# Two heads on the two halves of the array: float32 attention products reordered beside long split products

## The chip, the core and the metric

The kernel runs as one program on one core of a Trainium2 chip. TensorE multiplies (in the trace PE, with its weight loads as PEld), VectorE (DVE) and ScalarE (ACT) do the elementwise work, GpSimd (POOL) and SyncE (SP, which issues DMAs) help. The metric is the device time of one execution in microseconds: the median of three timed runs. A second, separate execution was profiled; all rows below come from that one.

## The reference, cut to what matters

Two transformer blocks with 256 tokens and a model width of 2048. The first block (run for two layers) mixes a state-space scan with an attention of eight heads, whose queries and keys have a part of 128 and a rotary part of 64; the scores are the sum of both parts:

```
q = jnp.concatenate([q[..., :MLA_NOPE], apply_rope(q[..., MLA_NOPE:], cos, sin)], axis=-1)   # 128 + 64
s = jnp.einsum('bqhd,bkhd->bhqk', q[:, q0:kend], k[:, :kend]) * scale     # causal, blocks of 128 queries
outs.append(jnp.einsum('bhqk,bkhd->bqhd', p, v[:, :kend]))
```

The second block has a branch with 16 query heads of width 64 in four key groups. Its output is a gated sum of three attentions:

```
o_cmp = jnp.einsum('bsgrc,bcgd->bsgrd', p_cmp, vc)         # over 15 block summaries per group
o = g[..., 0:1] * o_cmp + g[..., 1:2] * o_sel + g[..., 2:3] * o_win
```

With 256 tokens the selected blocks and the window each cover every causal key, so `o_sel` and `o_win` are plain causal attentions over two sets of keys and values. A second branch of that block, with heads of width 128, is not touched.

## The kernel before, in words

**Long products.** Nearly all work is products of the 256 tokens with weights of width 2048 and more. Weights and activations are split into a high and a low part; `block` (L423 to L425) issues three products of 128x512 for every slice of 128 rows, `block_fm` (L461 to L463) three of 128x256. A weight tile arrives by DMA (`raw`), ACT makes its high part `wh` (L411), DVE its low part `wl` (L412). There are five `raw` buffers and four of `wh` and of `wl`; these steps are put far ahead of the others by priority.

**Tasks.** The rest is written as generators that the long products advance: `tick` is called every six products of `block`, and each task then issues its next step and says how many ticks it wants to wait (`yield n`). PE's order is exactly the order in which the program is written out this way; DVE, ACT and POOL are ordered by a scheduler with priorities.

**Attention of a head.** `scores` (L665) writes the scores of the two query tiles into one PSUM bank `[128, 384]`: 256 keys for the second tile, 128 for the first. `soft` (L627 to L633) makes the exponentials from it: DVE writes `z`, ACT the exponential `e`, and `scaled` (L647) applies 1/sum and the gate. `probs_t` (L653 to L655, copied by ACT at L657) transposes `e`. Then the values' products. `z`, `e` and the transposed probabilities are tiles of a ring of nine buffers, `t2`; the PSUM banks `mb` are a ring of four.

**The two users that change.** `mla_heads` (first block, four pairs of heads in each of two layers) issues the scores of head 0 in one tick and those of head 1 in the next; per query tile a product over 128 rows (`qn`, `kk`) and one over 64 rows (`rp`, rows 0 to 63 for head 0, 64 to 127 for head 1). `branch_a_heads` (second block, eight chunks of two heads, a new chunk every seven ticks) issues four scores over 64 rows in four ticks: head 0 with both key sets, then head 1. For each head then follow two transposes, two ticks later four products of 64 columns of values (L1493, L1494), and one product of 15 rows, the block summaries (L1496).

**How the trace names it.** A float32 product of the program appears as two passes, each with its own weight load: L665 with `kt,qt` is issued 64 times and has 128 records. A form such as `64*128 64x256` reads: weights of 64 rows by 128 columns, a moving operand of 64 rows by 256 columns.

Of the kernel before, what the change touches and what calls it, by code (L numbers as in the profile page):

```python
# [15 lines left out]
OP = mybir.AluOpType  # L16
# [3 lines left out]
P = 128  # L20
# [14 lines left out]
# ---------------------------------------------------------------- host layout  # L35
# [6 lines left out]
def _tile_a(w, width=512):  # L42
    """[L, K, N] -> [L, N/width, K/512, 2, 128, 2, width]; one [128, 2, width] block per transfer."""
    L, K, N = w.shape
    w = w.reshape(L, K // 512, 2, 2, P, N // width, width)
    return np.ascontiguousarray(w.transpose(0, 5, 1, 2, 4, 3, 6))


def _tile_b(w):
    """[L, 2048, N] -> [L, N/128, 2, 128, 8, 128]."""  # L50
    L, K, N = w.shape
    w = w.reshape(L, 2, 8, P, N // P, P)
    return np.ascontiguousarray(w.transpose(0, 4, 1, 3, 2, 5))


def _cols(v):
    """[n*128] -> [128, n]"""
    return v.reshape(-1, P).T


def _rows(v):
    """[n] -> [128, n], the same row on every partition"""
    return np.broadcast_to(v.reshape(1, -1), (P, v.size))


def _feature_major(x):
    """[256, 2048] -> [128, 16, 256]"""
    return np.ascontiguousarray(x.T.reshape(16, P, S).transpose(1, 0, 2))


def _token_major(x):
    """[256, n] -> [128, 2, n]"""
    return np.ascontiguousarray(x.reshape(2, P, -1).transpose(1, 0, 2))
# [19 lines left out]
def _head_order_a():  # L93
    """Position p of a query head of branch a: pairs (g, g + 1) of key groups with one r."""
    return [(2 * (c // 4) + i) * 4 + c % 4 for c in range(8) for i in range(2)]
# [64 lines left out]
def _layout(a):  # L160
    """Every array that goes to the chip, in the order and the shape it is read."""
    o = {}
# [11 lines left out]
    L = DEPTH  # L174
# [48 lines left out]
# ---------------------------------------------------------------- the program  # L223


class _Task:
    """Work beside the long products, cut into steps; a step yields the number of ticks to wait."""
# [5 lines left out]
class _Net:  # L233
# [29 lines left out]
    # -- tasks  # L263
# [17 lines left out]
    def get(self, t):  # L281
        """the result of a task, a list of them, or the value itself"""
        if isinstance(t, _Task):
            while not t.done:
                self.tick()
            return t.result
        return t
# [6 lines left out]
    # -- small things  # L294
# [30 lines left out]
    def rsqrt(self, out, ss, width):  # L325
        """out = (ss / width + eps) ** -0.5"""
# [9 lines left out]
    def squares(self, src, acc):  # L336
        """acc = sum of src ** 2 along the free axis"""
        self.nc.scalar.activation(self.junk[:, :src.shape[1]], src, AF.Square, accum_out=acc)

    def head_squares(self, src, acc, heads):  # L340
        """acc [128, heads] = sum of squares of every head's columns of src [128, 512]"""
# [4 lines left out]
    # -- operands of the long products  # L346
# [6 lines left out]
    def hi_lo(self, pair, c, n, src, gain=None, imm=None):  # L353
        """chunks c .. c+n of a pair from src [128, n, 256], times a gain by partition"""
# [17 lines left out]
    def two_transposed(self, srcs):  # L372
        """srcs: two functions of the token tile giving [128 tokens, 128]; a bank [128, 2, 256]"""
# [9 lines left out]
    def transposed(self, src, gain=None, imm=None):  # L383
        """src(m) -> [128 tokens, 512]; a task for its four chunks, feature-major, as a pair"""
# [8 lines left out]
    def weights(self, src, n, w):  # L393
        """one block [128, n, w] from DRAM, split into high and low parts"""
# [19 lines left out]
    def block(self, pairs, srcs, w=512, hold=HOLD):  # L414
        """token-major products: two banks [128 tokens, w]; the last weights serve one bank, then the other"""
# [35 lines left out]
    def block_fm(self, pairs, src):  # L451
        """feature-major products for 128 columns: one bank [128 features, 256 tokens]"""
# [15 lines left out]
    # -- the residual stream  # L468
# [24 lines left out]
    # -- start  # L493

    def start(self):
        """the first operands, in the order they are needed"""
# [44 lines left out]
    def angles(self):  # L541
        """cosines and sines of every rotary embedding"""
# [45 lines left out]
    def rope_gains(self, l, which):  # L588
        """rotary tables with the gain of the rotated part folded in"""
# [12 lines left out]
    def rotate(self, out, x, ct, st):  # L602
        """out, x [128, ..., 2 * half] (up to three free axes), tables broadcast to the same shape"""
# [12 lines left out]
    # -- attention of one head  # L616

    def soft(self, s, mask, scale_of, spans):
        """spans [(lo, hi)] by query tile over the columns of a bank; returns exp and 1/sum"""
# [29 lines left out]
    def probs_t(self, e):  # L649
        """probabilities [128, 384] transposed: keys by [tile 0: all tokens | tile 1: second half]"""  # L650
# [9 lines left out]
    def scores(self, s, parts):  # L660
        """s [128, 384]; parts [(qT [k, 256], kT [k, 256])] sum over the contraction"""
        nc = self.nc
        for m, (a, b) in reversed(list(enumerate(self.CAUSAL))):
            for i, (q, k) in enumerate(parts):
                nc.tensor.matmul(s[:, a:b], lhsT=q[:, m * P:(m + 1) * P], rhs=k[:, 0:b - a],  # L665
                                 start=(i == 0), stop=(i == len(parts) - 1))

    # ------------------------------------------------------------ block 1
# [72 lines left out]
    def rms_bank(self, r):  # L741
        """a column by token tile, as rows on every partition"""
# [13 lines left out]
    def ssd_steps(self, l, krd):  # L756
        """softplus of the step sizes, and the decays by step"""
# [48 lines left out]
    def ssd_scan(self, l, cb, dt, a):  # L806
# [24 lines left out]
        # masked c . b, state positions on the partitions  # L831
# [9 lines left out]
        # state after the first chunk  # L841
# [19 lines left out]
        def decays(m, g):  # L861
            """rows of summed decays for 8 heads"""
# [84 lines left out]
    def mla_queries(self, l, qa_t, rqa):  # L947
        """[nope heads 0-3, nope heads 4-7, rope of all heads] before the norm; -scale/rms by (tile, head)"""
# [68 lines left out]
    def mla_heads(self, l, hp, q, nsc, kn, kr, v):  # L1017
        """two heads: chunks of the pair that four heads share"""
# [12 lines left out]
        es = []  # L1031
        for j in range(2):
            h = hp * 2 + j
            s = self.bank([P, 384])
            b = slice(j * 64, j * 64 + 64)
            self.scores(s, [(qn[:, j], kk[:, j]), (rp[b, 0], rp[b, 1])])
            e, rc = self.soft(s, self.causal, lambda m: nsc[:, m, h:h + 1], self.CAUSAL)
            self.scaled(e, rc)
            es.append(e)
            yield 1  # L1040
        yield 3
# [15 lines left out]
    # -- attention to the memory  # L1057
# [34 lines left out]
    def head_rms(self, t, name):  # L1092
        """t [128, 2, 512]: 1/rms by (tile, head of 128)"""
# [84 lines left out]
    # -- feed forward  # L1178
# [45 lines left out]
    # ------------------------------------------------------------ block 2  # L1224
# [29 lines left out]
    def x_fm(self, nb):  # L1254
        """512 features of x times their gain, feature-major"""
# [9 lines left out]
    def h2_pair(self, nb, xt, rb):  # L1265
        """512 features of rms(x) * g_pre * (1 + scale) + shift"""
# [19 lines left out]
    def rope_part(self, t, c0, heads, dh, rot, tabs):  # L1286
        """rotate the first rot of every head's dh columns of t[:, :, c0:...] in place"""
# [3 lines left out]
    def gate_fm(self, pairs, src):  # L1291
        """twice silu of 4 feature-major chunks"""
# [10 lines left out]
    def plain_t(self, src, out):  # L1303
        """out [128, 4, 256] = four chunks of src(m), feature-major"""
# [5 lines left out]
    def summaries(self, t, c0, which, vc):  # L1310
        """block summaries of the columns c0.. (4 groups of 64) of t: [128 (group, 32), 64]"""
# [70 lines left out]
    def branch_a_inputs(self, pairs):  # L1382
# [11 lines left out]
        # a quarter of 1 + tanh: the gate, halved against the doubled silu  # L1394
# [7 lines left out]
    def branch_a_cmp(self, tasks, qt, ga, kcr):  # L1402
        """probabilities over the block summaries, gated: [128 (group, 32), r, tokens]"""
        nc = self.nc
        for t in tasks:
            yield from self.after(t)
        x = kcr[:, 0:16].unsqueeze(1)
# [50 lines left out]
    def branch_a_heads(self, c, kts, qt, ks, kt, ga, cmp, vcr, zf):  # L1458
        """the two query heads of chunk c"""
# [9 lines left out]
        for i in range(2):  # L1469
            g = 2 * gp + i  # L1470
            b = slice(i * 64, i * 64 + 64)
            for br in range(2):
                s = self.bank([P, 384])
                self.scores(s, [(qt[gp][b, r], kt[b, 2 * br + gp])])
                e, rc = self.soft(s, self.causal, lambda m: -0.125, self.CAUSAL)
                f = self.small([P, 2], name="fa")
                nc.vector.tensor_tensor(f, rc, ga[:, :, (br + 1) * 16 + r * 4 + g], op=OP.mult)
                self.scaled(e, f)
                es[i, br] = e
                yield 1  # L1480
        yield 1
        o = self.bank([P, S])
        for i in range(2):
            g = 2 * gp + i
            b = slice(i * 64, i * 64 + 64)
            vs = slice(256 + g * 64, 256 + (g + 1) * 64)
            pts = []
            for br in range(2):
                pts.append(self.probs_t(es[i, br]))
                yield 1  # L1490
            yield 1
            for br, t in enumerate(ks):
                nc.tensor.matmul(o[b], lhsT=t[:, 0, vs], rhs=pts[br][:, 0:256], start=(br == 0), stop=False)  # L1493
                nc.tensor.matmul(o[b, P:], lhsT=t[:, 1, vs], rhs=pts[br][:, 256:384], start=False, stop=False)  # L1494
            cs = slice(g * 32, g * 32 + 15)
            nc.tensor.matmul(o[b], lhsT=vcr[cs], rhs=pct[cs, r], start=False, stop=True)  # L1496
# [6 lines left out]
    def branch_b(self, pairs, nb):  # L1503
        """inputs of 4 heads"""
# [8 lines left out]
    def branch_b_heads(self, h, q, k, v, zf):  # L1513
# [9 lines left out]
        self.scores(s, [(qk[:, 0], qk[:, 1])])  # L1523
# [16 lines left out]
    def gate_rows(self):  # L1540
        """gate * g_post along the free axis"""
# [13 lines left out]
    def hybrid(self, xt, r):  # L1555
# [7 lines left out]
        vcr = self.small([P, 64], name="vcr", bufs=1)  # L1563
        qt, qts = [], []
# [9 lines left out]
        cmp = self.spawn(self.branch_a_cmp(qts + [cmp], qt, ga, kcr), 1)  # L1574
        za = [self.gate_fm(pairs, I["w2_za"][0, c:c + 4]) for c in (0, 4)]
        oa = [self.spawn(self.branch_a_heads(c, kts, qt, ks, kt, ga, cmp, vcr, za), 1 + A_LAG * c) for c in range(8)]
# [101 lines left out]
```

## Time and profile before

| what | value |
|---|---|
| median of three timed runs | 3197.31 us (3196.97 to 3197.81) |
| profiled execution, first to last instruction (its span) | 3196.7 us; the page gives no other time for it |
| PE busy | 3175.3 us, 99% of the span, 15705 matmul records |
| PE weight loads busy | 2656.9 us |
| DVE, ACT, POOL busy | 2034.1, 1553.8, 53.4 us |
| mean granted clock | 0.998 of 2.4 GHz |

A PE that is busy all the time is not a PE at its peak: a matmul's recorded time includes the part in which the next one already streams. What a product costs in a row of products is the distance from its start to the next start, and the rows below are read that way.

### The profile page before, as it was taken

What the parts mean: (1) busy time and instruction counts of PE and PEld (TensorE: products, weight loads), DVE (VectorE), ACT (ScalarE), POOL (GpSimd) and SP (SyncE); (2) the same over time, 40 slices, a digit from 0 to 9 for tenths busy, and PEclk for the clock granted to TensorE, in tenths of its full rate; (3) what the DMA queues carried; (4) which work ended last, traced back from release to release, by engine and by line L of the source; (5) the groups of instructions that cost most, each with busy time, mean ns of one, the idle gap of its engine ahead of it and who ended that gap; (6) DMA issues with size and microseconds to landing.
All of it is one profiled execution on the core that took longest, in us unless ns stands there. A gap on an engine that the chain in (4) does not pass through costs nothing.

```text
span 3196.7 us, 41513 instructions
## 1 busy us (share of the span) xinstructions
PE 3175.3 (99%) x15705; PEld 2656.9 (83%) x15705; DVE 2034.1 (64%) x3015; ACT 1553.8 (49%) x2191; POOL 53.4 (2%) x77
## 2 busy tenths in 40 slices
PE   9999999999999999999999999999999999999998
PEld 8987888888888889887888888888878977888887
DVE  6886665555555566885767677766765555455554
ACT  7465564444444455474654444444454455444443
POOL 0010000000000000010000000000000000000000
PEclk9999999999999999999999999999999999999999
DMA  8554555555555556454567777777746533555454
GB/s 299 172 169 145 186 172 187 192 192 191 192 187 192 191 175 189 159 183 141 190 228 265 266 270 270 253 250 269 269 143 219 174 105 99 179 184 180 162 184 151
DMA packets 175160, 625.28 MB, mean 196 GB/s; under 512 B 19696, under 2 KB 19952, under 8 KB 174704
## 3 DMA queue, kind: packets, MB, share of 16 engines
q1 hardware_dynamic: 173952, 620.26, 58.2%
q8 instruction: 123, 2.02, 0.3%
q10 hardware_dynamic: 1008, 2.37, 0.2%
q14 instruction: 77, 0.63, 0.1%
HBM read 620.46 MB, written 2.10 MB: 195 GB/s over the span
## 4 chain that ended last, share of the span: by engine, by line
PE 96%; DVE 1%; DMA 1%; issue 1%; POOL 0%; ACT 0%; SPq 0%; DVEq 0%; POOLq 0%; ACTq 0%
PE pw L423 27%; PE pw L425 27%; PE pw L424 27%; PE pw L461 2%; PE pw L462 2%; PE pw L463 2%; PE mb L377 2%; PE mb L665 2%; DMA wada<-w_ada 1%; PE mb L1493 1%; PE mb L1346 0%; PE mb L903 0%; DVE wl L412 0%; PE mb L1496 0%; PE mb L887 0%
## 5 line engine op out<-in xcount | busy, mean ns | idle before, releaser
L412 DVE TENSOR_TENSOR wl<-raw,wh 128x1024 fp32r<-128x1024 f32 (+3 forms) x1069 | 1285.6, 1204 | 969.7 <-ACT wh L411 967.2
L411 ACT ACTIVATE wh<-raw 128x1024 fp32r<-128x1024 f32 (+3 forms) x1069 | 1114.9, 1043 | 1384.8 <-PE pw L425 1258.0
L423 PE MATMUL pw<-wh,xh 128*128 128x512 f32 (+2 forms) x3952 | 1555.4, 394 | 6.2 <-ACT wh L411 4.9
L425 PE MATMUL pw<-wh,xl 128*128 128x512 f32 (+2 forms) x3952 | 1526.3, 386 | 0.0
L424 PE MATMUL pw<-wl,xh 128*128 128x512 f32 (+2 forms) x3952 | 1524.6, 386 | 0.6 <-DVE wl L412 0.6
L423 PEld LDWEIGHTS pw<-wh,xh 128*128 128x128 f32 x3952 | 744.2, 188 | 153.3 <-ACT wh L411 4.9
L425 PEld LDWEIGHTS pw<-wh,xl 128*128 128x128 f32 x3952 | 743.1, 188 | 150.7 <-DVE xl L368 0.7
L424 PEld LDWEIGHTS pw<-wl,xh 128*128 128x128 f32 x3952 | 744.6, 188 | 141.6 <-DVE wl L412 2.1
L461 PE MATMUL pw<-xh,wh 128*128 128x256 f32 x640 | 183.2, 286 | 0.0
L463 PE MATMUL pw<-xh,wl 128*128 128x256 f32 x640 | 181.2, 283 | 0.0
L462 PE MATMUL pw<-xl,wh 128*128 128x256 f32 x640 | 181.1, 283 | 0.0
L485 DVE TENSOR_TENSOR x<-x,pw 128x512 f32<-128x512 f32 x224 | 144.9, 679 | 3.8 <-PE pw L425 3.8
L1240 DVE CUSTOM_DVE_ANT_0 wada<-wada,crow 128x1024 f32<-128x1024 f32 x96 | 117.3, 1221 | 33.9 <-DMA wada<-w_ada 33.8
L461 PEld LDWEIGHTS pw<-xh,wh 128*128 128x128 f32 x640 | 122.7, 192 | 1.3 <-issue 0.8
L462 PEld LDWEIGHTS pw<-xl,wh 128*128 128x128 f32 x640 | 122.8, 192 | 0.1
L463 PEld LDWEIGHTS pw<-xh,wl 128*128 128x128 f32 x640 | 122.7, 192 | 0.0
L630 ACT ACTIVATE t<-t,mn 128x256 f32<-128x256 f32 (+1 forms) x128 | 58.4, 457 | 63.1 <-DVE mn L627 62.3
L367 ACT ACTIVATE xh<-mb,par 128x256 fp32r<-128x256 f32 x112 | 50.9, 467 | 13.1 <-PE mb L377 12.2
L368 DVE SCALAR_TENSOR_TENSOR xl<-mb,par,xh 128x256 fp32r<-128x256 f32 x112 | 51.8, 478 | 3.7 <-ACT xh L367 2.6
L334 POOL TENSOR_TENSOR xr<-rs,mhalf 128x1 f32<-128x1 f32 x16 | 9.8, 619 | 2512.1 <-DVE rs L330 2306.4
L358 ACT ACTIVATE xh<-mb 128x512 fp32r<-128x512 f32 (+1 forms) x68 | 35.1, 516 | 30.5 <-PE mb L377 15.8
L627 DVE CUSTOM_DVE_ANT_0 t<-mb,cst 128x128 f32<-128x128 f32 x80 | 26.0, 354 | 25.8 <-PE mb L665 25.4
(358 smaller groups left out, 1564.4 us busy)
## 6 DMA issues: line engine op xcount, KB each, us to landing
raw<-w_gate SPq DMA_DIRECT2D x176, 512.0 KB, 3.6
raw<-w_up SPq DMA_DIRECT2D x176, 512.0 KB, 3.8
raw<-w_down SPq DMA_DIRECT2D x176, 512.0 KB, 3.6
raw<-w_out SPq DMA_DIRECT2D x96, 512.0 KB, 3.5
wada<-w_ada SPq DMA_DIRECT2D x96, 512.0 KB, 5.5
raw<-w_in_x SPq DMA_DIRECT2D x48, 512.0 KB, 3.9
raw<-w_in_z SPq DMA_DIRECT2D x32, 512.0 KB, 3.5
raw<-w_ma SPq DMA_DIRECT2D x32, 512.0 KB, 3.3
```

The source lines that it names most:

```text
L377: self.nc.tensor.transpose(t[:, j, m * P:(m + 1) * P], src(m), self.ident)
L411: nc.scalar.activation(h, raw, AF.Copy)
L412: nc.vector.tensor_tensor(l, raw, h.bitcast(F32), op=OP.subtract)
L423: nc.tensor.matmul(pt[m], lhsT=xh[:, k, ms], rhs=wh[:, j], start=c == 0, stop=False)
L424: nc.tensor.matmul(pt[m], lhsT=xh[:, k, ms], rhs=wl[:, j], start=False, stop=False)
L425: nc.tensor.matmul(pt[m], lhsT=xl[:, k, ms], rhs=wh[:, j], start=False, stop=c == 4 * n - 1)
L461: nc.tensor.matmul(pt, lhsT=h[:, j], rhs=xh[:, c], start=(k == 0), stop=False)
L462: nc.tensor.matmul(pt, lhsT=h[:, j], rhs=xl[:, c], start=False, stop=False)
L463: nc.tensor.matmul(pt, lhsT=l[:, j], rhs=xh[:, c], start=False, stop=(k == 15))
L485: self.nc.vector.tensor_tensor(xs, xs, pt[m], op=OP.add)
L665: nc.tensor.matmul(s[:, a:b], lhsT=q[:, m * P:(m + 1) * P], rhs=k[:, 0:b - a], start=(i == 0), stop=(i == len(parts) - 1))
L1240: nc.vector.tensor_tensor_reduce(out=t, in0=t, in1=self.crow[hf], scale=1.0, scalar=0.0, op0=OP.mult, op1=OP.add, accum_out=self.adap[:, j ...
```

## The change

`scores` takes a list of heads and alternates them: for each part, for each query tile, first the product of head 0, then that of head 1, into two banks. `mla_heads` calls it once for both heads, so that the four products over 128 rows stand together and the four over 64 rows behind them; one tick of waiting goes to the end (`yield 5`). `branch_a_heads` calls it once for each of the two key sets with both heads. Its values' products of the two heads alternate between the output partitions 0 to 63 and 64 to 127. The block summaries' values become one product over 128 rows and 128 columns: `vcb` holds, for each pair of groups, the summaries' values in a matrix that is zero elsewhere (two GpSimd fills, four DVE copies; its buffers are the ones of `qct` and `qst` of the first block). Docstrings and comments went too.

```
-    def scores(self, s, parts):
-        for m, (a, b) in reversed(list(enumerate(self.CAUSAL))):
-            for i, (q, k) in enumerate(parts):
-                nc.tensor.matmul(s[:, a:b], lhsT=q[:, m * P:(m + 1) * P], rhs=k[:, 0:b - a],
-                                 start=(i == 0), stop=(i == len(parts) - 1))
+    def scores(self, heads):
+        n = len(heads[0][1])
+        for i in range(n):
+            for m, (a, b) in reversed(list(enumerate(self.CAUSAL))):
+                for s, parts in heads:
+                    q, k = parts[i]
+                    nc.tensor.matmul(s[:, a:b], lhsT=q[:, m * P:(m + 1) * P], rhs=k[:, 0:b - a],
+                                     start=(i == 0 and m == 1), stop=(i == n - 1 and m == 0))
...
 mla_heads
+        ss = [self.bank([P, 384]) for _ in range(2)]
+        bs = [slice(j * 64, j * 64 + 64) for j in range(2)]
+        self.scores([(ss[j], [(qn[:, j], kk[:, j]), (rp[bs[j], 0], rp[bs[j], 1])]) for j in range(2)])
         for j in range(2):
             h = hp * 2 + j
-            s = self.bank([P, 384])
-            b = slice(j * 64, j * 64 + 64)
-            self.scores(s, [(qn[:, j], kk[:, j]), (rp[b, 0], rp[b, 1])])
...
-            yield 1
-        yield 3
+        yield 5
...
 branch_a_cmp
+        for t in vcb:
+            nc.gpsimd.memset(t, 0.0)
...
+        for g in range(4):
+            cs = slice(g * 32, g * 32 + 15)
+            nc.vector.tensor_copy(vcb[g // 2][cs, g % 2], vcr[cs])
...
 branch_a_heads
+        for br in range(2):
+            ss = [self.bank([P, 384]) for _ in range(2)]
+            self.scores([(ss[i], [(qt[gp][bs[i], r], kt[bs[i], 2 * br + gp])]) for i in range(2)])
+            for i in range(2):
+                e, rc = self.soft(ss[i], self.causal, lambda m: -0.125, self.CAUSAL)
...
+            yield 2
+        yield 1
+        pts = {}
+        for br in range(2):
+            for i in range(2):
+                pts[i, br] = self.probs_t(es[i, br])
                 yield 1
         yield 1
         o = self.bank([P, S])
...
+        nc.tensor.matmul(o, lhsT=vcr[gp].rearrange("p a d -> p (a d)"), rhs=pct[:, r], start=True, stop=False)
+        for br, t in enumerate(ks):
+            for k in range(2):
+                for i in range(2):
+                    vs = slice(256 + (2 * gp + i) * 64, 256 + (2 * gp + i + 1) * 64)
+                    nc.tensor.matmul(o[bs[i], k * P:], lhsT=t[:, k, vs],
+                                     rhs=pts[i, br][:, 256 * k:256 + 128 * k], start=False, stop=(br == 1 and k == 1))
```

On PE, the scores of the first pair of heads of the first layer, before (two heads, six long products between them; numbers tell the buffers apart):

```order
L665 MATMUL mb_2709<-t2_2641,t2_2640 128x256
L665 MATMUL mb_2709<-t2_2642 128x256
L665 MATMUL mb_2709<-t2_2641,t2_2640 128x128
L665 MATMUL mb_2709<-t2_2642 128x128
...
L665 MATMUL mb_2738<-t2_2641,t2_2640 128x256
L665 MATMUL mb_2738<-t2_2642 128x256
```

The same place in the changed program (`t2_2642` holds the rotary parts, the products over 64 rows):

```order
L669 MATMUL mb_2709<-t2_2641,t2_2640 128x256
L669 MATMUL mb_2710<-t2_2641,t2_2640 128x256
L669 MATMUL mb_2709<-t2_2641,t2_2640 128x128
L669 MATMUL mb_2710<-t2_2641,t2_2640 128x128
L669 MATMUL mb_2709<-t2_2642 128x256
L669 MATMUL mb_2710<-t2_2642 128x256
L669 MATMUL mb_2709<-t2_2642 128x128
L669 MATMUL mb_2710<-t2_2642 128x128
```

Before, products over 128 and 64 rows follow each other in turn, four runs of each for the pair; now there is one run of each.

On PE, the first values' products of the second block's branch, before, with the scores and transposes that stand around them:

```order
L1493 MATMUL mb_21733<-t2_21738,ks_20784 64x256
L1494 MATMUL mb_21733<-t2_21738,ks_20784 64x128
L1493 MATMUL mb_21733<-t2_21756,ks_21013 64x256
L1494 MATMUL mb_21733<-t2_21756,ks_21013 64x128
L1496 MATMUL mb_21733<-pct_21322,vcr_19859 64x256
L653 MATMUL mb_21798<-cst_88,t2_21679 128x128
L654 MATMUL mb_21798<-cst_88,t2_21679 128x128
L655 MATMUL mb_21798<-cst_88,t2_21679 128x128
L665 MATMUL mb_21804<-kt_20558,qt_20015 128x256
L665 MATMUL mb_21804<-kt_20558,qt_20015 128x128
```

The same place in the changed program, with the end of the next chunk's scores ahead (six long products left out):

```order
L669 MATMUL mb_21836<-kt_20560,qt_20017 128x256
L669 MATMUL mb_21835<-kt_20560,qt_20017 128x128
L669 MATMUL mb_21836<-kt_20560,qt_20017 128x128
...
L1497 MATMUL mb_21881<-pct_21330,qct_19860 128x256
L1502 MATMUL mb_21881<-t2_21745,ks_20786 64x256
L1502 MATMUL mb_21881<-t2_21763,ks_20786 64x256
L1502 MATMUL mb_21881<-t2_21745,ks_20786 64x128
L1502 MATMUL mb_21881<-t2_21763,ks_20786 64x128
L1502 MATMUL mb_21881<-t2_21775,ks_21015 64x256
L1502 MATMUL mb_21881<-t2_21827,ks_21015 64x256
L1502 MATMUL mb_21881<-t2_21775,ks_21015 64x128
L1502 MATMUL mb_21881<-t2_21827,ks_21015 64x128
```

One group of nine products now serves both heads of a chunk; it stands behind the scores of the next chunk, whose softmax takes the next buffers of the `t2` ring.

On DVE, that softmax in the changed program (the steps from the exponential's sum to `scaled` left out):

```order
L412 TENSOR_TENSOR wl_22008<-raw_22006,wh_22007 128x1024 [waits DMAHW7_49,Activation_49]
L627 ISA t2_21841,mn_21843<-mb_21835,cst_88 128x128 [waits PE_49]
...
L627 ISA t2_21855,mn_21857<-mb_21836,cst_88 128x128 [waits PE_49]
...
L1505 TENSOR_TENSOR t1_21891<-mb_21881,zf_21024 128x256 [waits PE_49]
...
L412 TENSOR_TENSOR wl_22074<-raw_22072,wh_22073 128x1024 [waits DMAHW0_49,Activation_49]
```

and one of before, where only one head's softmax stands between two `wl`:

```order
L412 TENSOR_TENSOR wl_22001<-raw_21999,wh_22000 128x1024 [waits DMAHW7_49,Activation_49]
L627 ISA t2_21836,mn_21838<-mb_21833,cst_88 128x256
L627 ISA mn_21838 128x1
L627 ISA t2_21865,mn_21867<-mb_21862,cst_88 128x128 [waits PE_49]
L627 ISA mn_21867 128x1
```

Nine places back in the ring from `t2_21855` stands `t2_21763`, one of the transposed probabilities that the nine products of PE read.

## Rows read from the trace of the kernel before

**Rows 1.** The page, parts 1 and 4: engines' busy time; the chain by engine.

```profile
PE 3175.3 (99%) x15705; PEld 2656.9 (83%) x15705; DVE 2034.1 (64%) x3015; ACT 1553.8 (49%) x2191; POOL 53.4 (2%) x77
PE 96%; DVE 1%; DMA 1%; issue 1%; POOL 0%; ACT 0%; SPq 0%; DVEq 0%; POOLq 0%; ACTq 0%
```

**Rows 2.** Waits of PE: for whom, us in total, times, longest.

```profile
PE pw L423 <- ACT wh L411: 4.9, 1, 4.9
PE pw L424 <- DVE wl L412: 0.6, 2, 0.4
```

**Rows 3.** PE by line and form: count, busy us, mean ns, idle before.

```profile
L665 PE MATMUL mb<-kt,qt 64*128 64x256 f32 x64 | 22.3, 428 | 0.0
L1493 PE MATMUL mb<-t,ks 128*64 128x256 f32 x64 | 19.9, 392 | 0.0
...
L665 PE MATMUL mb<-t 64*128 64x256 f32 x32 | 11.1, 429 | 0.0
...
L1496 PE MATMUL mb<-pct,vcr 15*64 15x256 f32 x32 | 10.3, 400 | 0.0
```

**Rows 4.** Timeline of PE, one 64-row score: start us, length us, instruction.

```profile
2572.22 0.40 PE L425 MATMUL pw<-wh,xl 128*128 128x512 f32 x1
2572.55 0.92 PE L665 MATMUL mb<-kt,qt 64*128 64x256 f32 x4
2573.40 0.50 PE L423 MATMUL pw<-wh,xh 128*128 128x512 f32 x1
2573.73 0.40 PE L424 MATMUL pw<-wl,xh 128*128 128x512 f32 x1
2573.97 0.39 PE L425 MATMUL pw<-wh,xl 128*128 128x512 f32 x1
```

**Rows 5.** Timeline of PE, one head's values and the transposes behind.

```profile
2574.66 0.39 PE L425 MATMUL pw<-wh,xl 128*128 128x512 f32 x1
2574.98 0.65 PE L1493 MATMUL mb<-t,ks 128*64 128x256 f32 x2
2575.46 0.38 PE L1494 MATMUL mb<-t,ks 128*64 128x128 f32 x2
2575.68 0.59 PE L1493 MATMUL mb<-t,ks 128*64 128x256 f32 x2
2576.11 0.38 PE L1494 MATMUL mb<-t,ks 128*64 128x128 f32 x2
2576.42 0.64 PE L1496 MATMUL mb<-pct,vcr 15*64 15x256 f32 x2
2577.00 0.33 PE L653 MATMUL mb<-cst,t 128*128 128x128 f32 x1
2577.16 0.27 PE L654 MATMUL mb<-cst,t 128*128 128x128 f32 x1
```

**Rows 6.** Timeline of PE, one head's scores in the first block.

```profile
240.69 0.59 PE L665 MATMUL mb<-t,t 128*128 128x256 f32 x2
241.22 0.70 PE L665 MATMUL mb<-t 64*128 64x256 f32 x2
241.84 0.49 PE L665 MATMUL mb<-t,t 128*128 128x128 f32 x2
242.26 0.48 PE L665 MATMUL mb<-t 64*128 64x128 f32 x2
242.68 0.51 PE L423 MATMUL pw<-wh,xh 128*128 128x512 f32 x1
243.02 0.40 PE L424 MATMUL pw<-wl,xh 128*128 128x512 f32 x1
```

**Rows 7.** Windows: stretch, then busy us of engines, clock, DMA.

```profile
2558.00:2722.00 164.00, 164.00 (x833) 120.50 (x833) 91.67 (x314) 85.21 (x206) 0.00 (x0) 1.00 0.31 101
```

**Rows 8.** Windows with a low clock, and behind it.

```profile
2369.30:2375.90 6.60, 5.60 (x13) 4.35 (x14) 5.57 (x12) 2.80 (x7) 1.19 (x2) 0.50 0.09 32
2376.00:2382.60 6.60, 6.60 (x30) 5.45 (x29) 5.23 (x9) 4.64 (x8) 0.00 (x0) 1.00 0.22 57
```

More of the change, by code (lines that the diff above doesn't have):

```diff
@@ L1031, in mla_heads @@
         es = []
+        ss = [self.bank([P, 384]) for _ in range(2)]
+        bs = [slice(j * 64, j * 64 + 64) for j in range(2)]
+        self.scores([(ss[j], [(qn[:, j], kk[:, j]), (rp[bs[j], 0], rp[bs[j], 1])]) for j in range(2)])
         for j in range(2):
             h = hp * 2 + j
-            s = self.bank([P, 384])
-            b = slice(j * 64, j * 64 + 64)
-            self.scores(s, [(qn[:, j], kk[:, j]), (rp[b, 0], rp[b, 1])])
-            e, rc = self.soft(s, self.causal, lambda m: nsc[:, m, h:h + 1], self.CAUSAL)
+            e, rc = self.soft(ss[j], self.causal, lambda m: nsc[:, m, h:h + 1], self.CAUSAL)
             self.scaled(e, rc)
             es.append(e)
-            yield 1
-        yield 3
+        yield 5
         pts = []
@@ L1400, in compressed, with branch_a_cmp @@
         yield from self.summaries(kc, 256, "cv", vcr)
-    def branch_a_cmp(self, tasks, qt, ga, kcr):
+    def branch_a_cmp(self, tasks, qt, ga, kcr, vcr, vcb):
         nc = self.nc
+        for t in vcb:
+            nc.gpsimd.memset(t, 0.0)
         for t in tasks:
             yield from self.after(t)
+        for g in range(4):
+            cs = slice(g * 32, g * 32 + 15)
+            nc.vector.tensor_copy(vcb[g // 2][cs, g % 2], vcr[cs])
         x = kcr[:, 0:16].unsqueeze(1)
@@ L1468, in branch_a_heads @@
         es = {}
[L1469 to L1475, printed above, removed]
+        bs = [slice(i * 64, i * 64 + 64) for i in range(2)]
+        for br in range(2):
[3 more added lines that the diff above has]
+                e, rc = self.soft(ss[i], self.causal, lambda m: -0.125, self.CAUSAL)
                 f = self.small([P, 2], name="fa")
-                nc.vector.tensor_tensor(f, rc, ga[:, :, (br + 1) * 16 + r * 4 + g], op=OP.mult)
+                nc.vector.tensor_tensor(f, rc, ga[:, :, (br + 1) * 16 + r * 4 + 2 * gp + i], op=OP.mult)
                 self.scaled(e, f)
                 es[i, br] = e
+            yield 2
[4 more added lines that the diff above has]
+                pts[i, br] = self.probs_t(es[i, br])
                 yield 1
@@ L1482, in branch_a_heads @@
         o = self.bank([P, S])
[L1483 to L1496, printed above, removed]
+        nc.tensor.matmul(o, lhsT=vcr[gp].rearrange("p a d -> p (a d)"), rhs=pct[:, r], start=True, stop=False)
[5 more added lines that the diff above has]
+                                     rhs=pts[i, br][:, 256 * k:256 + 128 * k], start=False, stop=(br == 1 and k == 1))
         y = self.t1([P, 1, S])
@@ L1522, in branch_b_heads @@
         s = self.bank([P, 384])
-        self.scores(s, [(qk[:, 0], qk[:, 1])])
+        self.scores([(s, [(qk[:, 0], qk[:, 1])])])
         e, rc = self.soft(s, self.dilated, lambda m: -(128.0 ** -0.5), self.CAUSAL)
@@ L1563, in hybrid @@
         vcr = self.small([P, 64], name="vcr", bufs=1)
+        vcb = [self.small([P, 2, 64], name=n, bufs=1) for n in ("qct", "qst")]
         qt, qts = [], []
@@ L1573, in hybrid @@
         ks, kt, kts = self.branch_a_keys(pairs)
-        cmp = self.spawn(self.branch_a_cmp(qts + [cmp], qt, ga, kcr), 1)
+        cmp = self.spawn(self.branch_a_cmp(qts + [cmp], qt, ga, kcr, vcr, vcb), 1)
         za = [self.gate_fm(pairs, I["w2_za"][0, c:c + 4]) for c in (0, 4)]
-        oa = [self.spawn(self.branch_a_heads(c, kts, qt, ks, kt, ga, cmp, vcr, za), 1 + A_LAG * c) for c in range(8)]
+        oa = [self.spawn(self.branch_a_heads(c, kts, qt, ks, kt, ga, cmp, vcb, za), 1 + A_LAG * c) for c in range(8)]
         b0 = self.branch_b(pairs, 0)
```

## The prediction

> **What bounds the kernel now.** I read the page's busy times and its chain first: PE is busy for 3175.3 of 3196.7 us, and the chain that ends last runs 96% through PE [rows 1]. Then the waits of PE: the longest is one of 4.9 us at the start, and for DVE's low weights it waits 0.6 us in the whole program [rows 2]. So time that PE saves is time saved, unless it then finds weights missing. The question is what the changed products cost on PE, and that is not in the groups of [rows 3]: a mean of 428 ns for a 64-row pass holds the overlap with the next one. The timeline gives it, from start to start.
>
> **What a pass costs.** Between products of one shape, two passes of 256 columns take 2576.11 - 2575.68 = 0.43 us and two of 128 take 2575.68 - 2575.46 = 0.22 [rows 5]; I use 0.215 and 0.108 for one. An undisturbed long product of 512 columns takes 0.23 to 0.24 (the last two of [rows 4]); I use 0.23.
>
> **What a change of shape costs.** A 64-row score stands between two long products [rows 4]. From L425 at 2572.22 to L424 at 2573.73 are 1.51 us. The four passes are 0.65 and the two long products 0.23 each, together 1.11. The other 0.40 is lost: 0.10 ahead of the score and 0.10 inside it, 0.09 behind it and 0.11 in the long product after it. That is 0.20 for a change into 64 rows and 0.20 for the one back. The first block shows the same, four times for one head [rows 6]: the product over 128 rows lasts 0.53 to the next start where two passes need 0.43, the 64-row one 0.62, then 0.42 and 0.42 where 0.22 would do, and 0.34 for the long product; the excess is 0.80, again 0.20 a change. For 64 columns [rows 5]: in, 0.09 (2574.66 to 2574.98 against 0.23) and 0.05 (L1493, 0.48 against 0.43); to the 15-row summaries 0.09 and 0.05; back to the transposes 0.10 and 0.05. That is about 0.145 a change; back to a long product I take 0.20 from rows 4.
>
> The Trainium skill, "TensorEngine Tiling (Array Packing)", section "Tiling Modes", says that a change of tiling mode, though not a change of tile within one mode, drains the engine. The trace agrees for the mode (0.20 and 0.145 us); a change of tile within a mode is in no row here.
>
> **The sum without any overlap.**
> - First block: four changes for each of 16 heads before, 64 in all; after, two for a pair, 16. 48 x 0.20 = 9.6 us.
> - Scores of the second block: 32 visits of PE before (64 passes of 256 columns in rows 3, two for a visit), 16 after, each with a change in and out: 16 x 0.40 = 6.4.
> - Values: 16 visits before with three changes, half of them followed by transposes (0.43) and half by long products (0.49): 7.4. After, 8 visits; the summaries' product is over the whole array, so only one change in and one out: 8 x 0.345 = 2.8. Saved 4.6.
> - Summaries: 32 passes of 256 columns [rows 3] become 16: 16 x 0.215 = 3.4.
>
> Together 24.0 us. This part needs nothing new: fewer changes of kinds that the rows show, fewer passes of a kind that they show.
>
> **The overlap of the halves.** The alternation can bring more if the two halves work side by side. No row shows two halves next to each other, so I bound it. Below: nothing, or a loss if going from half to half costs like a change of shape (a rival). Above: half of the passes' time. A visit of two 64-row scores has four passes of 256 and four of 128, 1.30 us in a row; there are 24 (8 pairs of the first block, 16 in the second). A visit of values has 2.59 us; there are 8. Half of all is 24 x 0.65 + 8 x 1.30 = 26.0. I take less, because a float32 product is two passes in the same half, so the order is A1 A2 B1 B2 a1 a2 b1 b2 (capitals 256 columns). Let starts stay in order and a half do one pass at a time: A1 at 0, A2 and B1 at 0.215, B2 and a1 at 0.43, a2 at 0.54, b1 at 0.645, b2 at 0.755, end at 0.865. That saves 0.43 of 1.30. Of values two such groups follow each other, and the second begins beside b2: about 1.62 instead of 2.59, saved 0.97. So 24 x 0.43 + 8 x 0.97 = 18.1. I take this value although the nearest rows (two passes in one half, rows 5) show none: those passes share their half, and here the halves share neither rows nor banks in the scores, nor columns in the values.
>
> The Trainium skill, "TensorEngine Tiling (Array Packing)", section "Overview", gives up to a factor of two where a dimension is at most 64; the sum by that is the upper bound above. No run so far shows it.
>
> **What is hidden.** Two fills on POOL (53.4 us busy in all) and four small DVE copies stand before the first score that needs them, and DVE is busy for 91.67 of 164 us there [rows 7]. Softmax work is the same in amount; two heads' come at once. In the second block, the second softmax of a chunk now takes ring buffers that the values' products of the chunk before still read, and these stand one tick later on PE. DVE and ACT wait there, with a `wl` queued behind. From the scores to the end of those products are six long products (6 x 0.23 = 1.4), the summaries (0.43), two changes' worth (0.3) and at most 2.6: 4.7 us, seven times. I cost it at nothing, because the high-priority `wl` run ahead (four buffers) and PE waited 0.6 us for them before [rows 2]. If the cover is gone, it is the rival below. The two banks that a pair takes at once are ones released two ticks (twelve long products, 2.8 us) earlier.
>
> **One term with no sign.** The clock stood at its lower level (1.2 GHz, 0.50) for some 6.6 us at 2369.3, behind PE's waits at the border of the blocks, and 13 matmuls started there instead of 30 [rows 8]: 17 x 0.23, about 3.8 us. All work after about 236 us moves by a few us, and I can't say whether the dip stays: plus or minus 3.8.
>
> **Forecast.** 24.0 + 18.1 = 42.1 us off the profiled span of 3196.7; the median of the runs, 3197.3, is 0.6 above it, and I keep that: 3155.2, say 3155. Own range 3149 to 3161, for the clock and for a sixth of the overlap.
>
> **Rivals.**
> - The halves don't overlap; the alternation only reorders. Nothing in the trace speaks against it: float32 passes have only been seen one after the other. 3197.3 - 24.0 = 3173.
> - Only one kind overlaps. The rows' halves write to two banks, the columns' halves to one, so one may work and the other not: 3197.3 - 24.0 - 10.3 = 3163 (scores), or 3197.3 - 24.0 - 7.8 = 3165 (values).
> - The full half, if passes of both halves run together all the time: 3197.3 - 50.0 = 3147. Against it stands the order of passes.
> - Each step from half to half costs what a change of shape costs, so the alternation gives back what the grouping saved. Three steps in 24 visits at 0.20 and seven in 8 at 0.145: 14.4 + 8.1 = 22.5; 3197.3 - 24.0 + 22.5 = 3196, no change. For it: no row shows such a step for free. Against: the rows lose time where the shape of the weights changes, not where products of one shape follow each other.
> - Slower: the ring. DVE stands at the second softmax until PE is through the values' products, the next `wl` waits behind it, and PE runs out of weights. If all of it reached PE without overlap, 7 x 4.7 = 33, and 3197.3 - 24.0 + 33 = 3206. It decides from 24.0 / 7 = 3.4 us of waiting per chunk. Against: the stretch has DVE idle for 44% [rows 7], and of 4.7 us the buffered weights cover several products of 0.23 each.
>
> **How the numbers follow.** Forecast 0.54, no overlap 0.25, one kind only 0.09, full half 0.04, steps that cost 0.05, the ring 0.03. To hold 8 in 10 the range has to reach the case without overlap: 3147 to 3177 (3173 and the clock's 3.8). What a measurement of this kernel can tell from no change is about 0.2%, 6.4 us, here. Faster by more: the first four, 0.92; within: 0.05; slower: 0.03.
>
> **What would show it.** The grouping: 64-row products in 24 runs of four (L669) with one loss of 0.20 at each end, none between the two heads. The overlap: in a visit, almost no distance from the start of the second pass to that of the third, and of the fourth to the fifth, and about 0.87 us from the first start to the last pass's end, against 1.30. The values: L1502 in 8 runs of eight, about 1.6 us long. The ring: PE's waits for `wl` at L424 stay under 2 us. The forecast is wrong if the starts within a visit stay at 0.215 and 0.108 throughout (no overlap), if each switch of half adds 0.1 or more, or if DVE's wait shows up in PE's.

## The result, and the profile after

The changed kernel takes 3147.47 us (median of 4 runs, 3147.17 to 3147.81), beside 3197.41 for the kernel before in the same runs: 49.9 us less, a ratio of 0.9844 with a 95% interval of 0.983 to 0.9858. That is 7.5 us below the forecast of 3155 and within half a microsecond of the rival "full half" (3147). It is inside the wide range (3147 to 3177) by 0.5 us, and outside the prediction's own range (3149 to 3161). Its profiled span is 3145.4 us, 51.3 below the 3196.7 of the kernel before.

The page after, the engines' busy times and the chain by engine:

```profile
PE 3124.6 (99%) x15689; PEld 2634.9 (84%) x15689; DVE 2033.2 (65%) x3019; ACT 1548.2 (49%) x2191; POOL 53.8 (2%) x79
PE 97%; DVE 1%; issue 1%; ACT 1%; POOL 0%; DMA 0%; SPq 0%; DVEq 0%; POOLq 0%; ACTq 0%
```

PE lost 50.7 us of busy time and is still busy for 99% of the span; DVE and ACT do what they did. The waits of PE after, the first and the one for DVE's low weights:

```profile
PE pw L423 <- ACT wh L411: 4.5, 1, 4.5
...
PE pw L424 <- DVE wl L412: 0.7, 2, 0.5
```

They answer to [rows 2] and are as they were: no new wait took the place of the time saved.

The groups of [rows 3] after, by line and form (count, busy us, mean ns, idle before):

```profile
L669 PE MATMUL mb<-kt,qt 64*128 64x256 f32 x64 | 11.2, 428 | 0.0
L1502 PE MATMUL mb<-t,ks 128*64 128x256 f32 x64 | 10.0, 392 | 0.0
...
L669 PE MATMUL mb<-t 64*128 64x256 f32 x32 | 5.6, 428 | 0.0
...
L1497 PE MATMUL mb<-pct,qct 128*128 128x256 f32 x8 | 2.4, 378 | 0.0
```

As many passes as before, each as long as before (428 and 392 ns), but the time in which any of them runs has halved: 22.3 to 11.2, 19.9 to 10.0, 11.1 to 5.6 us. A mean that stays while the union halves means two at a time.

The timeline of PE, the scores of the first pair of heads in the first block (start us, length us), answers to [rows 6]:

```profile
240.47 0.40 PE L425 MATMUL pw<-wh,xl 128*128 128x512 f32 x1
240.71 1.47 PE L669 MATMUL mb<-t,t 128*128 128x256 f32 x8
242.10 0.92 PE L669 MATMUL mb<-t 64*128 64x256 f32 x8
242.96 0.50 PE L423 MATMUL pw<-wh,xh 128*128 128x512 f32 x1
```

Eight 64-row passes last 0.92 us, to the next start 0.86. In [rows 4] four passes last 0.92, to the next start 0.85. So the second head's scores cost 0.01 us. The same stretch cut to its first 0.05 us, and the group of this form in the window from 242.10 to 242.113 (count, busy us, mean ns, idle before):

```profile
242.10 0.49 PE L669 MATMUL mb<-t 64*128 64x256 f32 x2
...
L669 PE MATMUL mb<-t 64*128 64x256 f32 x2 | 0.5, 480 | 0.0
```

Two passes have started, and both are over within 0.49 us, where one lasts 0.48. Their starts are 7 ns apart in the trace's records. The values of the first chunk, which answer to [rows 5]:

```profile
2561.01 0.40 PE L425 MATMUL pw<-wh,xl 128*128 128x512 f32 x1
2561.24 0.59 PE L1497 MATMUL mb<-pct,qct 128*128 128x256 f32 x2
2561.76 1.52 PE L1502 MATMUL mb<-t,ks 128*64 128x256 f32 x16
2563.22 0.50 PE L423 MATMUL pw<-wh,xh 128*128 128x512 f32 x1
2563.55 0.39 PE L424 MATMUL pw<-wl,xh 128*128 128x512 f32 x1
```

Sixteen passes take 1.46 us to the next start, of which about 0.15 are changes of shape (0.05 in, 0.10 out). The eight passes of a single head in rows 5 took 1.44 to the start of the summaries.

The dip of the clock [rows 8] is half as long in this profile; the windows on it and behind it:

```profile
2355.90:2359.10 3.20, 3.20 (x8) 2.52 (x9) 3.20 (x8) 1.26 (x3) 0.00 (x0) 0.50 0.00 0
2359.30:2362.50 3.20, 3.20 (x16) 2.63 (x15) 1.71 (x3) 2.55 (x5) 0.00 (x0) 1.00 0.00 0
```

Eight matmuls in place of 16: about 1.8 us lost. The prediction counted 3.8 in [rows 8], but PE was busy for only 5.60 of those 6.60 us; at half the clock that is 2.8 us lost, and the other 1.0 us PE stood waiting. The shorter dip is thus about 1 us of the profile's 51.3. Of the timed runs the record has the mean granted clock alone, 0.999 in one and 0.998 in three, and their times lie within 0.6 us.

### The profile page after: what moved, and what is told of

Same layout as the page of the kernel before. It is cut to its first block, busy times and chain, and to the rows that moved or that the text cites. A ratio compares the mean times of both kernels' runs of the same rounds, so it can differ in the third digit from the quotient of the medians.

```text
span 3145.4 us, 41489 instructions
## 1 busy us (share of the span) xinstructions
PE 3124.6 (99%) x15689; PEld 2634.9 (84%) x15689; DVE 2033.2 (65%) x3019; ACT 1548.2 (49%) x2191; POOL 53.8 (2%) x79
## 4 chain that ended last, share of the span: by engine, by line
PE 97%; DVE 1%; issue 1%; ACT 1%; POOL 0%; DMA 0%; SPq 0%; DVEq 0%; POOLq 0%; ACTq 0%
PE pw L423 28%; PE pw L425 27%; PE pw L424 27%; PE pw L461 2%; PE pw L462 2%; PE pw L463 2%; PE mb L377 2%; PE mb L669 1%; PE mb L1349 0%; PE mb L907 0%; PE mb L1502 0%; DVE wl L412 0%; PE mb L891 0%; DMA s<-x_fm 0%; PE mb L1160 0%
## 5 line engine op out<-in xcount | busy, mean ns | idle before, releaser
L425 PE MATMUL pw<-wh,xl 128*128 128x512 f32 (+2 forms) x3952 | 1525.4, 386 | 0.1
L425 PEld LDWEIGHTS pw<-wh,xl 128*128 128x128 f32 x3952 | 742.7, 188 | 151.1 <-DVE xl L368 0.7
L359 DVE TENSOR_TENSOR xl<-mb,xh 128x512 fp32r<-128x512 f32 (+1 forms) x68 | 39.2, 591 | 4.2 <-ACT xh L358 3.9
```

Source lines behind the costliest of these rows:

```text
L425: nc.tensor.matmul(pt[m], lhsT=xl[:, k, ms], rhs=wh[:, j], start=False, stop=c == 4 * n - 1)
```

## The experiments

After the result the theory was: the gain is 24.0 us for fewer changes of shape and summaries' passes, as in the prediction, and half of the passes' time, 26.0. The rivals: the parts lean on each other; the order and not the two halves makes the gain; and, on why more overlapped than forecast, three ideas of what the engine takes in order. "Before" is the kernel before on the same chip, in the same job; it took 3197.41 us beside the changed kernel and 3197.51 to 3198.03 in the other jobs, so a difference between two changed versions can carry 0.6 us of that. A visit is one stretch of PE on products of one shape: a visit of scores serves a pair of heads, a visit of values serves a chunk.

**The scores' part alone.** In `branch_a_heads` the values' half of the function is the one of before:

```
 # scores of both heads per key set, as changed; then, as before:
+for i in range(2):
+    pts = [...]     # this head's two transposes
+    for br, t in enumerate(ks):
+        nc.tensor.matmul(o[b], lhsT=t[:, 0, vs], rhs=pts[br][:, 0:256], ...)
+        nc.tensor.matmul(o[b, P:], lhsT=t[:, 1, vs], rhs=pts[br][:, 256:384], ...)
+    nc.tensor.matmul(o[b], lhsT=vcr[cs], rhs=pct[cs, r], start=False, stop=True)
```

> The scores' part of the change alone: pairs of heads in the scores as in the changed kernel; the values and the block summaries as before, head by head. Theory (savings of the two parts add up, each being fewer changes of shape plus half of the passes' time): 9.6 + 6.4 for changes and 24 x 0.65 for the overlap, 31.6 us, so 3197.4 - 31.6 = 3165.8. Rival (the two parts lean on each other, for instance through the buffer ring or the clock): the savings of this run and of the values alone differ from 49.9 together by more than 3 us.

Measured 3166.39 (3166.17 to 3166.81), before 3197.98; ratio 0.9902 (0.9887 to 0.9917): 31.6 us less, as worked out.

**The values' part alone.** `scores` is called for one head at a time, in the ticks of before; the values as changed:

```
+        for m, (a, b) in reversed(list(enumerate(self.CAUSAL))):
+            for i in range(n):
...
+            self.scores([(s, [(qt[gp][b, r], kt[b, 2 * br + gp])])])
...
+                yield 1
```

> The values' part alone: scores head by head in their own ticks as before; the values' products of two heads alternate and the summaries are one full product. Theory: 4.6 for changes of shape, 3.4 for the summaries' passes, 8 x 1.30 for the overlap, 18.4 us, so 3197.4 - 18.4 = 3179.0. Rival: as for the scores alone, a sum with that run other than 49.9.

Measured 3177.88 (3176.86 to 3178.71); ratio 0.9939 (0.9922 to 0.9955): 20.1 us less, 1.7 more than worked out. Together the two parts give 51.7 where the whole change gave 49.9. The difference is under the 3 us that were set, and each interval reaches some 5 us to either side, so the parts add up as far as this can tell. The excess of 1.7 us is not explained: each of the eight visits of values takes 1.45 us to the next start, as in the changed kernel. In this profile the dip of the clock is a short one, as in the profile after (0.50 from 2369.3 to 2372.6, 1.00 from 2373.0 on); whether that made the excess is not shown.

**Heads in turn.** The same products, without the alternation in a visit:

```
-            for m, (a, b) in reversed(list(enumerate(self.CAUSAL))):
-                for s, parts in heads:
+            for s, parts in heads:
+                for m, (a, b) in reversed(list(enumerate(self.CAUSAL))):
...
+        for i in range(2):
             for br, t in enumerate(ks):
                 for k in range(2):
-                    for i in range(2):
```

> As the changed kernel, but within a visit first all products of head 0, then all of head 1 (scores: 256 and 128 columns of head 0, then of head 1; values: all four of head 0, then of head 1). The same products, the same changes of shape. Theory 1 (a product of two passes is the unit: products start in program order, each as soon as its half is free): a visit of scores takes 1.08 us instead of 0.65, of values 2.37 instead of 1.30: 3147.5 + 24 x 0.43 + 8 x 1.08 = 3166. The first product of head 1 starts with the 128-column product of head 0. Theory 2 (each half takes its own work whatever the order): 3147.5. Theory 3 (a single pass is the unit, as in the prediction): 1.19 and 2.49 us, 3147.5 + 24 x 0.54 + 8 x 1.19 = 3170.

Measured 3153.89 (3153.43 to 3154.05); ratio 0.9862 (0.9848 to 0.9877). That is 6.4 us over the changed kernel, and none of the three theories gave it. The timeline tells why. Scores of the first pair: the whole visit, a window from 242.36 to 242.53 in it, and the group by form in that window:

```profile
242.01 0.93 PE L669 MATMUL mb<-t 64*128 64x256 f32 x8
242.87 0.50 PE L423 MATMUL pw<-wh,xh 128*128 128x512 f32 x1
...
242.01 0.71 PE L669 MATMUL mb<-t 64*128 64x256 f32 x4
...
L669 PE MATMUL mb<-t 64*128 64x256 f32 x4 | 0.7, 428 | 0.0
```

The visit is as short as with the alternation (0.86). In the window all four passes of 256 columns, those of both heads, have started, and no pass of 128 columns; in the program the 128-column product of head 0 stands ahead of the 256-column one of head 1. So the product of head 1 overtook one that was waiting for its half; its first pass starts 13 ns after the first of head 0. Theories 1 and 3 fall here. But the values, four products of a head in turn, are longer, and two windows from 2563.30, to 2563.36 and to 2563.37, show where head 1 comes in:

```profile
2562.66 2.22 PE L1502 MATMUL mb<-t,ks 128*64 128x256 f32 x16
2564.81 0.50 PE L423 MATMUL pw<-wh,xh 128*128 128x512 f32 x1
...
2562.93 0.60 PE L1502 MATMUL mb<-t,ks 128*64 128x256 f32 x3
...
2562.93 0.87 PE L1502 MATMUL mb<-t,ks 128*64 128x256 f32 x5
```

Until 2563.36, 0.70 us after the visit's start, only head 0 has worked; then two passes start within 0.01 us, its third product's first and head 1's first. At that moment one product of head 0 runs and one waits. Theory 2 falls too. The visit is 2.15 to the next start instead of 1.46; 8 x 0.69 = 5.5 of the 6.4 us. What fits both is that a half takes one running and one waiting product, and that only a third one holds up what stands behind it.

**Both heads in one half.** Head 1's scores read rows 0 to 63 and its values go to partitions 0 to 63, but for the last product; the second head's own scores and most of its own values are left out:

```
-[(qt[gp][bs[i], r], kt[bs[i], 2 * br + gp])]
+[(qt[gp][bs[0], r], kt[bs[0], 2 * br + gp])]
...
+last = br == 1 and k == 1
+nc.tensor.matmul(o[bs[i if last else 0], k * P:], lhsT=t[:, k, vs],
```

> As the changed kernel, but both heads of a pair use the same half: rows 0 to 63 for the scores of both, and output partitions 0 to 63 for the values of both but for the last product of head 1 (so the second head's scores and values are not its own here). The grouping stays, the overlap goes. Theory: only the 24.0 us of the grouping remain, less the one pair of products that may still overlap: 3197.4 - 24.0 - 8 x 0.22 = 3171.6; starts within a visit 0.215 and 0.108 apart. Rival (the gain comes from the order alone, not from two halves): 3147.5.

Measured 3171.65 (3170.76 to 3172.11); ratio 0.9918 (0.9903 to 0.9933). The eight passes of the first block's visit in one half, and the first visit of values:

```profile
242.20 1.57 PE L669 MATMUL mb<-t 64*128 64x256 f32 x8
243.70 0.50 PE L423 MATMUL pw<-wh,xh 128*128 128x512 f32 x1
...
2570.17 2.60 PE L1503 MATMUL mb<-t,ks 128*64 128x256 f32 x16
2572.70 0.50 PE L423 MATMUL pw<-wh,xh 128*128 128x512 f32 x1
```

The scores take 1.50 to the next start instead of 0.86, the values 2.53 instead of 1.46: with the halves gone, 0.64 and 1.07 of a visit come back, and 24 x 0.64 + 8 x 1.07 = 23.9 of the 24.2 us over the changed kernel. So the gain is split as worked out, 24.0 us for the grouping and the rest for two halves at once; the order alone doesn't make it.

**Three products in turn**, to test the theory of one running and one waiting product:

```
+for i, j in ((0, 0), (0, 1), (0, 2), (1, 0), (1, 1), (1, 2), (0, 3), (1, 3)):
+    br, k = j // 2, j % 2
```

> As the changed kernel, but a visit of values issues three products of head 0 (256, 128, 256 columns), three of head 1, then the last of each. Theory (a half takes one running and one waiting product, four passes, and what is issued behind waits until there is room; from the run with heads in turn): head 1 starts with the 128-column product of head 0, 0.43 us late, and the visit lasts 1.72 instead of 1.30: 3147.5 + 8 x 0.43 = 3150.9. Theory 1 of that run (a product waits for room in its half, and nothing behind it starts): head 1 starts with the third product, 0.65 late, the visit lasts 1.94, 3152.6. Theory 2 (halves independent without limit): 3147.5.

Measured 3151.48 (3150.86 to 3151.64); ratio 0.9855 (0.9841 to 0.987). The visit of the second chunk, then windows from 2578.30 to 2578.345 and to 2578.36:

```profile
2577.87 2.00 PE L1501 MATMUL mb<-t,ks 128*64 128x256 f32 x16
2579.80 0.50 PE L423 MATMUL pw<-wh,xh 128*128 128x512 f32 x1
...
2578.13 0.38 PE L1501 MATMUL mb<-t,ks 128*64 128x256 f32 x1
...
2578.13 0.65 PE L1501 MATMUL mb<-t,ks 128*64 128x256 f32 x3
```

At 2578.35, 0.48 us after the start, the second product of head 0 and the first of head 1 begin together, with the third of head 0 waiting. That is the place the theory named, with 0.05 of a change of shape in the 0.48; the visit is 1.93 instead of 1.46, and 8 x 0.47 = 3.8 of the 4.0 us measured.

**Summaries apart.** Two products of 15 rows in place of the full one:

```
-nc.tensor.matmul(o, lhsT=vcr[gp].rearrange("p a d -> p (a d)"), rhs=pct[:, r], start=True, stop=False)
+for i in range(2):
+    cs = slice((2 * gp + i) * 32, (2 * gp + i) * 32 + 15)
+    nc.tensor.matmul(o[bs[i]], lhsT=vcr[cs], rhs=pct[cs, r], start=True, stop=False)
```

> As the changed kernel, but the block summaries' values are two products of 15 rows by 64 columns again, next to each other at the start of a visit (other row strips, other column halves) in place of the one full product; no zero-filled matrix. Theory: the two run side by side like the other halves, 0.43 us together as the full product, and one more change of shape of 0.145 in each of 8 visits: 3147.5 + 1.2 = 3148.7. Rival: strips of 15 rows do not overlap: 3147.5 + 8 x (0.43 + 0.145) = 3152.1.

Measured 3148.4 (3147.99 to 3149.76); ratio 0.9846 (0.9829 to 0.9862), before 3197.51. The time can't tell the two apart by itself, the timeline does:

```profile
2562.29 0.40 PE L425 MATMUL pw<-wh,xl 128*128 128x512 f32 x1
2562.61 0.65 PE L1494 MATMUL mb<-pct,vcr 15*64 15x256 f32 x4
2563.19 1.52 PE L1499 MATMUL mb<-t,ks 128*64 128x256 f32 x16
```

Four passes last 0.65 us, as two do in rows 5 (L1496, 0.64): the 15-row strips run side by side as well. From L425 to the long product behind the values are 2.35 us, in the changed kernel 2.21 (2561.01 to 2563.22). The zero-filled full product therefore buys one change of shape a visit, 0.14 us, about 1 us in all, not the 3.4 us of passes: the alternation would have saved these too.

**Parts in turn.** In `scores` the loop over the query tiles goes outside again, the heads still alternate:

```
-        for i in range(n):
-            for m, (a, b) in reversed(list(enumerate(self.CAUSAL))):
+        for m, (a, b) in reversed(list(enumerate(self.CAUSAL))):
+            for i in range(n):
```

> As the changed kernel, but in the first block the parts alternate by query tile: two products over 128 rows, two over 64, again two over 128, two over 64. Two more changes of shape for each of 8 pairs. Theory: 16 x 0.20 = 3.2 us, 3150.7. Rival (a change of shape costs only at the ends of a visit): 3147.5.

Measured 3150.13 (3149.36 to 3150.8); ratio 0.9852 (0.9837 to 0.9866). By the time alone this is not clear of the changed kernel; the visit shows it:

```profile
241.18 0.39 PE L425 MATMUL pw<-wh,xl 128*128 128x512 f32 x1
241.41 1.02 PE L669 MATMUL mb<-t,t 128*128 128x256 f32 x4
242.37 0.70 PE L669 MATMUL mb<-t 64*128 64x256 f32 x4
243.00 0.71 PE L669 MATMUL mb<-t,t 128*128 128x128 f32 x4
243.64 0.49 PE L669 MATMUL mb<-t 64*128 64x128 f32 x4
244.06 0.50 PE L423 MATMUL pw<-wh,xh 128*128 128x512 f32 x1
```

From L425 to the long product behind the scores are 2.88 us; in the changed kernel 240.47 to 242.96, 2.49. Two more changes cost 0.39, 0.20 each.

**A lag of 8.** One number, `A_LAG`, from 7 to 8.

> As the changed kernel, with a new chunk of the second block's branch every 8 ticks in place of 7, so that a chunk's values stand right ahead of the next chunk's second scores, with no long product between them, and the buffer ring no longer makes that softmax wait for them. Theory: seven times one change of shape less, 7 x 0.20 = 1.4 us: 3146.1, too little to be told by the time, so the trace decides. Rival: the closer steps wait for banks, PE shows new waits, slower than 3147.5.

Measured 3146.17 (3145.35 to 3146.85); ratio 0.9839 (0.9824 to 0.9854). The second chunk's values and the scores behind them, with no long product between:

```profile
2577.95 1.52 PE L1502 MATMUL mb<-t,ks 128*64 128x256 f32 x16
2579.40 0.92 PE L669 MATMUL mb<-kt,qt 64*128 64x256 f32 x8
2580.25 0.50 PE L423 MATMUL pw<-wh,xh 128*128 128x512 f32 x1
```

One change (1.45 for the values' visit, as to a long product) serves where two stood; in this trace seven visits of values are followed by scores in this way, in the changed kernel none. Both kernels then ran in one job.

> The changed kernel as it is, beside the next run on the same chip. Both theories: 3147.5. It gives the number that the version with a lag of 8 has to beat.

> The version with a lag of 8 once more, in more rounds beside the changed kernel. Theory: 1.4 us below it (seven changes of shape). Rival: the 1.3 us seen between the two in different jobs were scatter, the two medians lie within 0.5 us.

The changed kernel took 3146.93 (3146.53 to 3148.45; ratio 0.9841, 0.9828 to 0.9855), the lag of 8 took 3145.51 (3144.89 to 3146.38; ratio 0.9837, 0.9823 to 0.985). The medians differ by 1.42 us, as worked out, and the runs don't overlap (3146.38 against 3146.53); the intervals of the ratios do. It is the best version measured, by a margin that only the traces make credible.

## Why the prediction was right, and what it mis-sized

- **PE sets the time, and what it saves is saved.** Right: the waits of PE are unchanged, and every run moved by what PE's visits moved by, to within 1.7 us.
- **0.20 us a change of shape, 0.145 for 64 columns, 24.0 us in all.** Right: with both heads in one half 26.3 us of the gain remained (3197.98 - 3171.65), of which 1.7 belong to the one pair of products that still overlapped, so 24.6. The bullet "Summaries" in it, 3.4 us for the full product, was right against the kernel before, but not a merit of the full product: the two small ones run side by side.
- **The halves work at once.** Right, for rows and for columns, in separate banks (scores) and in one (values). Whether two row halves could share a bank was not tried.
- **The size of the overlap, 18.1.** Too small; this is the term that failed. The step was "Let starts stay in order and a half do one pass at a time", with an order A1 A2 B1 B2. The runs show that starts don't stay in order: B1 starts 7 ns behind A1 instead of 0.215 us, and with heads in turn head 1's first product starts ahead of head 0's second. Then both halves are busy all the time: 24 x 0.65 + 8 x 1.30 = 26.0, the rival that had a chance of 0.04 ("Against it stands the order of passes"). That order was never in a row of the trace: the page shows two records for a product, and I took them for two things that start in turn. The measured return when the halves were taken away was 3171.65 - 3147.47 = 24.2, close to 26.0 less the 1.7 of the pair left in. Whether the engine takes a product whole or queues its two passes stays open: one running and one waiting product are also one running and three waiting passes, and no run here tells the two apart.
- **The range.** That the time lies inside 3147 to 3177 is luck: the margin of 0.5 us is less than the 0.6 us between the runs, and the prediction gives no reason for that lower end. Its own range, 3149 to 3161, missed.
- **The Trainium skill**, "TensorEngine Tiling (Array Packing)", section "Overview", gives up to a factor of two for a dimension of 64. Its sum was the upper bound, and the runs here agree with it: 0.86 us for eight passes and 0.85 for four. By the Trainium skill, "TensorE: Matmul & The Clock Gate", section "Part 3: Packing small matmuls — row/col tiling", matmuls start and end in program order. The run with heads in turn shows one that starts ahead of its place (13 ns behind the first pass of the visit, with a product before it still waiting), and there the measurement decides.
- **From half to half is free.** Right: 7 ns, no 0.20 or 0.145.
- **The ring and the closer softmaxes.** Right at nothing: 0.7 us of waits for `wl`, before 0.6.
- **The clock.** A term without sign, as forecast, but read too large: of the 3.8 us, 1.0 was PE's waiting and 2.8 the clock. The profile of the changed kernel has about half of the dip, and of the timed runs only the mean clock is known.

## What to carry to other kernels

Group products of one shape, since each change of shape on TensorE cost 0.14 to 0.20 us here, and let products over half of the rows or columns stand next to each other in different halves: the second was free. Strict alternation isn't needed for two products a head; with three or more of one half in a row the other half waits. Where a bound and a model of one's own lie 8 us apart and no row decides between them, 0.54 against 0.04 is too sure of the model.

## What the runs showed of the hardware

- Two float32 products in different halves start 7 ns apart when they alternate (two passes within 0.49 us, each 0.48 long), for 64 rows, 64 columns, and strips of 15 rows by 64 columns.
- A product can start ahead of one that precedes it in the program, if that one waits for its half; with one product running and two waiting in a half, nothing behind them started (heads and three in turn: 0.70 and 0.48 us after the visit's start). Whether the limit belongs to the half or to how far the engine looks past a waiting product, and whether it counts products or passes, was not told apart.
- A change of shape straight from 64 columns to 64 rows costs what one to a long product costs (1.45 and 1.46 us to the next start).
